# Two feed-forward openings re-ordered: a third pair by quarters, a down product set sooner, and t1, norm sums and one weight part at other times

## The chip, the cores and the metric

The kernel runs on one core of a Trainium2 chip. The metric is the device time of one execution in microseconds (us). Before the change it is 949.35 us, the median of three runs (948.52 to 949.43). Engines are called as in the profile: PE (matmul) with PEld (its weight loads), DVE (vector), ACT (scalar), POOL (GpSimd, which here issues the transfers that add), SP (which issues all other loads). Each engine works through its own queue in order.

## The reference

One block of an encoder over 512 positions and a width of 1024, in float32:

```python
h = x
h = h + 0.5 * swiglu(rmsnorm(h, g1), ffn1_w_in, ffn1_w_out)     # width 2816
z = rmsnorm(h, gm) @ w_in                                       # conv | q k v r | gate
h = h + concat([conv_module(z), gated_linear_attention(z)]) @ w_out
h = h + 0.5 * swiglu(rmsnorm(h, g2), ffn2_w_in, ffn2_w_out)     # width 2816
h = h + sigmoid(rmsnorm(h, gp) @ w_gate) * (p @ w_proj)
out = rmsnorm(h, gf)

def swiglu(x, w_in, w_out):
    gate, up = split(x @ w_in, 2)
    return (silu(gate) * up) @ w_out
```

The change is in the two feed-forward parts. "First layer" means the first of them (ffn1), "second layer" the other (ffn2).

## The kernel before

**Numbers in two parts.** Every operand of a matmul is split into a high part (rounded to fp32r by ACT: `high`, `act.copy`) and a low part (the remainder, a subtraction on DVE: `low`). A product takes three matmuls: high by high, high by low, low by high (`mm3`, `mul`). A weight tile of 128 x 1024 thus costs one ACT cast (wh) and one DVE subtraction (wl). `added` and `add_part` make the low part without DVE: ACT writes the negated high part, and a transfer issued by POOL adds the raw weight to it in memory.

**Pairs.** The 2816 columns of the gate and up projections are cut into 11 pairs of 256 (class `Left` holds the weights of one pair: raw tiles a11, a12 for the gate, a21, a22 for the up projection, each 4 of the 8 row blocks). A pair is computed in one of two ways. *Plain*: eight units h0 to h7 of 12 matmuls with 512 columns each (`plain_unit`). *By quarters*: the input rows and weights are cut in four, and seven products replace eight (`m1` to `m7`, 24 matmuls of 256 columns each). This takes sums of weights (s1 and s2 in `s12`, then `s3_`, `s4_`, all on DVE), parts of seven weight operands, and sums of the input called t1 to t4. The inputs' sums are made once per layer by `Right.steps`, and split once per layer in high and low by `Right.split`: two ACT casts and two DVE subtractions of 128 x 512 for each of t1, t2 and t3, and four of each at 128 x 256 for t4. m6 uses t2, m7 t3, m5 t1 and m4 t4.

**Down products.** The pairs' results go into the down projection by cuts of 4 column blocks (two pairs); the first cut takes blocks 0 to 3, thus pairs 0 and 1. A cut is four pieces of 24 matmuls with 512 columns (`second`, `piece`). Each piece works through its blocks in order, twice, and so needs the high and low parts of the activations (actH, actL, made in `act_parts`) of both pairs. An `act_parts` is emitted behind the unit after the pair's last one.

**Order of the work.** PE, DVE and ACT run in the order in which the program emits their instructions (`Ordered`, `in_order(True)`), so that a waiting instruction holds up everything behind it on its engine. In `ffn` a list of units is made (`units`, `add`, `due`), and `drive` walks through it: ahead of unit n it emits the jobs that units further on have asked for (fetches 7 to 9 units ahead, weight sums 6, weight parts `AHEAD` = 4), then the first left-over of the unit before, then the unit itself with its hook (`hooks`: here the splits of t1 to t4 and the steps of the input's sums hang), then the other left-overs. The raw weights, the wh and the wl have six buffers each, PSUM seven banks for this.

In the first layer pair 0 is computed at the kernel's start, pairs 1 and 2 are plain (`plain` = (1, 2)), and pairs 3 to 10 go by quarters. The list before starts

```text
h0..h7 of pair 1 | h0 h1 h2 | piece 0 | h3 | piece 1 | h4 h5 | piece 2 | h6 h7 | piece 3 (pair 2) | m1 3, m2 3, m1 4, m6 3, ...
```

and t2, t3, t1, t4 are split behind h5 and h7 of pair 1, h3 of pair 2 and m1 of pair 3. In the second layer pair 0 is plain and written out by hand ahead of `ffn` (`plain_block`: g0, u0, g1_, u1_, 24 matmuls each); between the blocks stand the input's sums, the norm (`norm.rows()`: eight tiny matmuls that sum the squares, then a chain over DVE and POOL), and the first parts of pair 1's weights. Pairs 1 to 10 go by quarters.

Of the kernel before, what the change touches and what calls it, by code (L numbers as in the profile page):

```python
# [62 lines left out]
def block_kernel(ctx: ExitStack, tc: tile.TileContext, a: dict, out: bass.AP):  # L63
# [29 lines left out]
    def tmp(s, w=SEQ, dt=F32, bufs=2):  # L93
        return tp.tile([P, w], dt, tag=s, bufs=bufs, name=nm(s))

    def bank():
        return pp.tile([P, SEQ], F32, tag="mm", bufs=7, name=nm("ps"))

    def aux():
        return pp.tile([P, SEQ], F32, tag="aux", bufs=1, name=nm("ax"))  # L100
# [108 lines left out]
    def mm3(ps, wh, wl, xh, xl, first, last):  # L209
        pe.matmul(ps, wh, xh, start=first, stop=False)  # L210
        pe.matmul(ps, wh, xl, start=False, stop=False)
        pe.matmul(ps, wl, xh, start=False, stop=last)
# [46 lines left out]
    def spread(col, copy=True):  # L259

        ps = aux()
        for j in range(TB):
            pe.transpose(ps[:, j * P:(j + 1) * P], col[:, j:j + 1].to_broadcast([P, P]), ident)
        if not copy:
            return ps
        bc = tmp("bc", bufs=1)
        act.copy(bc, ps)
        return bc
# [17 lines left out]
    class Norm:  # L286
# [5 lines left out]
        def add(self, h):  # L292
            if self.n == 0:
                act.activation(self.acc, h, AF.Square)
            else:
                sq = tmp("sq", bufs=3)
                act.activation(sq, h, AF.Square)
                self.engine.tensor_tensor(out=self.acc, in0=self.acc, in1=sq, op=ALU.add)
            self.n += 1
# [214 lines left out]
    w1 = Left(ffn1_in, 2)  # L514
# [9 lines left out]
    ps0 = [bank() for _ in range(4)]  # L524
    split_w(0, 1, dve.tensor_copy)
    split_x(0)
    mid = []
# [22 lines left out]
    xb = Right(hg, "ffn1_norm")  # L550
# [31 lines left out]
    AHEAD = 4  # L582
# [18 lines left out]
        for f in left:  # L601
            f()

    def ffn(w_in, w_out, x, gname, given, first, rsb, hooks, plain):


        norm = Norm()
# [3 lines left out]
        start = 1 + len(plain)  # L611
# [82 lines left out]
        def plain_unit(j):  # L694

            up, i, k = j // 4, j // 2 % 2, j % 2
            def run(p):
                if not j:
                    p.g, p.s = {}, {}
                if not k:  # L700
                    p.x = bank()
                ps = p.x
                wh, wl = p.part(f"a{1 + up}{1 + k}")
                cs = slice(i * P, (i + 1) * P)
                for c in range(4):
                    mm3(ps, wh[:, c, cs], wl[:, c, cs], *x.rows[4 * k + c], k == c == 0, k == 1 and c == 3)
                if not k:
                    return []
                if not up:
                    def gate():  # L710
                        p.s[i] = silu(scaled(ps, "g1"))
                    return [gate]
                return [lambda: gated_block(p, p.s[i], scaled(ps, "u1"), i),
                        lambda: act_parts(p) if i else None]
            return run
# [4 lines left out]
        def unit(kind, i):  # L720
            p = pairs[i]

            def go(run):
                left = run(p)
                hooks.get((kind, i), lambda *_: None)()
                return left

            if kind[0] == "h":
                j = int(kind[1])
                part, run = (f"a{1 + j // 4}{1 + j % 2}", plain_unit(j)) if j % 4 < 2 else (None, plain_unit(j))  # L730
                if part:
                    return [(AHEAD, lambda: p.part(part)), (9, lambda: p.fetch(part))], lambda: go(run)
            else:
                part, run = USES[kind]
            before = [(AHEAD + (kind == 'm5'), lambda: p.part(part))] if part else []
            if kind in ("m1", "m2"):
                before.append((7, lambda: p.fetch(part)))
            elif kind == "m6":
                before += [(9, lambda: p.fetch("a21", "a22")), (6, p.s12)]
            elif kind in ("m7", "m3"):  # L740
                before.append((6, p.s3_ if kind == "m7" else p.s4_))

            return before, lambda: go(run)
# [61 lines left out]
        units, had = [], set()  # L805

        def add(kind, i):
            if 0 <= i < npair and (kind, i) not in had:
                had.add((kind, i))
                units.append(unit(kind, i))  # L810

        cut_of = {f1 // 2 - 1: (f0, f1) for f0, f1 in CUTS}
        due = []
        for i in plain:
            for j in range(8):
                add(f"h{j}", i)
                if j in (2, 3, 5, 7):
                    units += due[:1]
                    due = due[1:]
            if i in cut_of:  # L820
                due += second(cut_of[i])
        for unit_ in (("m1", start), ("m2", start), ("m1", start + 1)):
            add(*unit_)
        for i in range(start, npair):
            add("m6", i)
            add("m7", i)
            add("m5", i)
            if i == end:
                half, rest = second(cut_of[i])
                units.append(half[0])  # L830
            else:
                add("m1", i + 1)
            add("m2", i + 1)
            units += due[:1]
            add("m4", i)
            add("m3", i)
            units += due[1:2]
            due = due[2:]
            if i in cut_of and i < end:
                due += second(cut_of[i])  # L840
        units += half[1:] + rest
# [18 lines left out]
    w_in = a["w_in"][0]  # L860
    w_ahead = []

    def sums_hooks(x, names, at):

        h = {}
        for name, key in zip(names, at):
            h[key] = lambda *_, name=name: x.split(name)
        return h

    hooks = sums_hooks(xb, ("t2", "t3", "t1", "t4"), (("h5", 1), ("h7", 1), ("h3", 2), ("m1", 3)))  # L870
    hooks.update({("h%d" % (i + 1), 1): f for i, f in enumerate(steps[2:])})
    hooks.update({("m5", 3): lambda *_: made[0](), ("m5", 4): lambda *_: constants(),
                  ("m4", 10): lambda *_: w_ahead.append(ahead(w_in, D_CONV, 2 * P)),
                  ("last", 4): lambda *_: w_ahead.append(ahead(w_in, 0, 2 * P))})
    hg, norm = ffn(ffn1_in, a["ffn1_w_out"][0], xb, "mix_norm", {0: Left(ffn1_in, 0), 1: w1},
                   (ps0[:2], ps0[2:]), lambda: spread(mid[0]), hooks, (1, 2))
    pool.on = False
    cw, gwu, mean, mask, nbias = made

# [61 lines left out]
    mid = []  # L941
# [10 lines left out]
    rs, rsb = mid  # L952
# [16 lines left out]
    for k0 in range(0, DC, 4):  # L969
        for i in range(2):  # L970
            for j in range(4):
                pe.matmul(ps[2 * RANK * j:2 * RANK * (j + 1)], gw[:, k0 + j, :], hg[k0 + j][i].bitcast(F32),
                          start=(k0 == i == 0), stop=(k0 + i == 5), skip_group_check=True)
# [339 lines left out]
    w0, w1 = wf[0], wf[1]  # L1313
# [40 lines left out]
    norm = Norm()  # L1354
# [36 lines left out]
    def turn_p(k):  # L1391
        ps = aux()
        for t in range(TB):
            pe.transpose(ps[:, t * P:(t + 1) * P], ptok[t][:, k * P:(k + 1) * P], ident)
        hi, lo = bt(F32R, "pTH"), bt(F32R, "pTL")
        act.copy(hi, ps)
        dve.tensor_tensor(out=lo, in0=ps, in1=hi.bitcast(F32), op=ALU.subtract)
        pT.append((hi, lo))
# [15 lines left out]
    def plain_block(p, up, i, mid={}):  # L1414
        ps = bank()
        cs = slice(i * P, (i + 1) * P)
        for k in range(DC):
            if k in mid:
                mid[k]()
            wh, wl = p.part(f"a{1 + up}{1 + k // 4}")  # L1420
            mm3(ps, wh[:, k % 4, cs], wl[:, k % 4, cs], *hg[k], k == 0, k == DC - 1)
        return ps

    mid = []
    xb = Right(hg, "ffn2_norm")
# [3 lines left out]
    w2 = wf[2]  # L1429
# [1 line left out]
    g0 = plain_block(w0, 0, 0)  # L1431
    steps[1]()
    steps[2]()
    u0 = plain_block(w0, 1, 0, {2: lambda: mid.append(norm.rows())})
    steps[3]()
    w1.add_part("a11", "a12")
    steps[4]()
# [1 line left out]
    g1_ = plain_block(w0, 0, 1, {1: lambda: mid.append(spread(mid[0]))})  # L1439
    xb.split("t2", "t3")  # L1440
    w1.part("s2")
    w1.s3_()
    w1.add_part("a22")
    u1_ = plain_block(w0, 1, 1)
    w1.part("s3")
    hooks = sums_hooks(xb, ("t1", "t4"), (("m1", 1), ("m2", 1)))
    hooks.update({("m7", 10): lambda *_: turn_p(0), ("m5", 10): lambda *_: turn_p(1)})

    w_gate = a["ple_w_gate"][0]
    q11, q21, q12, q22, b11, b21, t2, wproj = ([] for _ in range(8))  # L1450
# [59 lines left out]
    def todo(*fs):  # L1510
# [6 lines left out]
                  ("rest", 4): todo((q_high, b21, q21, 1), (first_sum, 1), (third_sum, 1)),  # L1517
                  ("rest", 6): todo((final_in,), (row_sums, 0))})
    hg, norm = ffn(ffn2_in, a["ffn2_w_out"][0], xb, "ple_norm", wf, ((g0, u0), (g1_, u1_)), mid[1], hooks, ())

    def of_rows(k, h):

        return [tuple(t[:, HS[h]] for t in hg[4 * k + c]) for c in range(4)]

    a11, a12, a21, a22 = of_rows(0, 0), of_rows(1, 0), of_rows(0, 1), of_rows(1, 1)
# [138 lines left out]
    def kept(ps, name, **kw):  # L1666
        o = tmp(name, **kw)
        act.copy(o, ps)
        return o
# [20 lines left out]
    t1, t3 = q11, q12  # L1690
    n2_ = [x for jp in range(2) for x in split_rows(n2, jp)]
    project(0)
    m1 = [kept(p_, "sq", bufs=3) for p_ in x_]
# [98 lines left out]
```

## Time and profile before

| | |
|---|---|
| median of three runs | 949.35 us |
| profiled execution | 949.29 us |
| its span, first to last instruction | 947.6 us |
| PE busy | 935.2 us (99%) |
| DVE busy | 758.0 us (80%) |
| ACT busy | 474.9 us (50%) |
| POOL busy | 55.4 us (6%) |
| mean granted PE clock | 0.998 |

In the timeline's rows the first number is the start in us, the second the time that the row covers, then engine, line, operation, tiles (out<-in), shapes, how many instructions are merged, and in square brackets the idle time before them and what ended it. Nearly all instructions are recorded at line 46, which is the helper that emits them, so they are told apart by tile names. A matmul's modelled duration overlaps the next one's; the rate is read from the starts.

### The profile page before, as it was taken

How to read it: one execution, taken by the hardware profiler on the slowest of the kernel's cores; microseconds unless marked ns; L12 is line 12 of the kernel's file. 1: busy time of each engine (PE TensorE's matmuls, PEld its weight loads, DVE VectorE, ACT ScalarE, POOL GpSimd, SP SyncE). 2: the span in 40 equal slices, each digit the busy share in tenths (PEclk: the TensorE clock that was granted, in tenths of full speed). 3: DMA queues.
4: the chain of work that ended last, by engine and by line, in shares of the span. 5: the costliest groups of instructions: out<-in, count | busy, mean ns of one | idle time of the engine just before them, and what ended most of it. 6: DMA issues, size and time to landing. Idle time of an engine off the chain costs nothing.

```text
span 947.6 us, 14550 instructions
## 1 busy us (share of the span) xinstructions
PE 935.2 (99%) x5842; PEld 831.2 (88%) x5842; DVE 758.0 (80%) x1032; ACT 474.9 (50%) x718; POOL 55.4 (6%) x70
## 2 busy tenths in 40 slices
PE   9999999999999999999999999999999999999996
PEld 7888999999999988788877789999999999998885
DVE  5876887887788566999986789887878787866896
ACT  5752544334443474463564865444434433445883
POOL 0000200000000110001120010000000000000121
PEclk9999999999999999999999999999999999999999
DMA  7532323342323593346552552432243224347463
GB/s 230 180 114 74 103 70 120 101 134 79 101 89 111 142 261 80 76 118 151 134 133 78 146 134 67 126 108 79 89 135 112 67 90 134 95 148 224 89 108 115
DMA packets 107543, 112.38 MB, mean 119 GB/s; under 512 B 5123, under 2 KB 96437, under 8 KB 107476
## 3 DMA queue, kind: packets, MB, share of 16 engines
q1 hardware_dynamic: 101732, 94.67, 32.3%
q0 software_dynamic: 5728, 16.78, 9.9%
q8 instruction: 46, 0.75, 0.3%
q14 instruction: 21, 0.17, 0.0%
q10 hardware_dynamic: 16, 0.00, 0.0%
HBM read 93.61 MB, written 2.10 MB: 101 GB/s over the span
## 4 chain that ended last, share of the span: by engine, by line
PE 96%; DVE 3%; ACT 1%; issue 0%; POOLq 0%; POOL 0%; DVEq 0%; ACTq 0%
PE ps L46 94%; PE ax L46 2%; DVE sqacc L46 1%; DVE wl L46 1%; DVE g L46 0%; DVE wr L46 0%; ACT wh L46 0%; DVE hgL L46 0%; ACT s L46 0%; DVE y L46 0%; DVE t1L L46 0%; POOLq L1788 0%; DVE actL L46 0%; ACT ycH L46 0%; ACT hgH L46 0%
## 5 line engine op out<-in xcount | busy, mean ns | idle before, releaser
L46 PE MATMUL ps<-hgH,wh 128*128 128x256 f32 (+1 forms) x768 | 235.8, 312 | 0.0
L46 PE MATMUL ps<-hgH,wl 128*128 128x256 f32 (+1 forms) x768 | 234.0, 310 | 0.9 <-DVE wl L46 0.9
L46 PE MATMUL ps<-hgL,wh 128*128 128x256 f32 (+1 forms) x768 | 234.2, 310 | 0.0
L46 DVE TENSOR_TENSOR wl<-wr,wh 128x1024 fp32r<-128x1024 f32 (+2 forms) x164 | 192.1, 1182 | 49.4 <-ACT wh L46 49.3
L46 ACT CAST wh<-wr 128x1024 fp32r<-128x1024 f32 (+2 forms) x177 | 177.8, 1019 | 32.8 <-PE ps L46 18.5
L46 PEld LDWEIGHTS ps<-hgH,wh 128*128 128x128 f32 x768 | 146.9, 191 | 9.9 <-issue 1.1
L46 PEld LDWEIGHTS ps<-hgH,wl 128*128 128x128 f32 x768 | 146.6, 191 | 8.7 <-DVE wl L46 1.1
L46 PEld LDWEIGHTS ps<-hgL,wh 128*128 128x128 f32 x768 | 146.3, 191 | 8.1 <-issue 0.2
L46 PE MATMUL ps<-actH,wh 128*128 128x512 f32 x352 | 137.4, 390 | 0.0
L46 PE MATMUL ps<-actL,wh 128*128 128x512 f32 x352 | 137.3, 390 | 0.0
L46 PE MATMUL ps<-actH,wl 128*128 128x512 f32 x352 | 136.9, 389 | 0.0
L46 ACT ACTIVATE s<-g 128x512 f32<-128x512 f32 x48 | 30.4, 633 | 196.1 <-DVE g L46 196.1
L46 DVE SCALAR_TENSOR_TENSOR cv<-glu,cw,cv 128x502 f32<-128x502 f32 (+24 forms) x120 | 81.0, 732 | 0.6
L46 PEld LDWEIGHTS ps<-actH,wl 128*128 128x128 f32 x352 | 66.1, 188 | 13.9
L46 PEld LDWEIGHTS ps<-actH,wh 128*128 128x128 f32 x352 | 66.2, 188 | 12.9
L46 PEld LDWEIGHTS ps<-actL,wh 128*128 128x128 f32 x352 | 66.2, 188 | 12.6
L46 DVE SCALAR_TENSOR_TENSOR h<-ps,h 128x512 f32<-128x512 f32 x80 | 54.0, 687 | 21.8 <-PE ps L46 21.8
L46 ACT COPY sq<-ps 128x512 f32<-128x512 f32 x40 | 23.3, 584 | 72.2 <-PE ps L46 72.2
L46 DVE TENSOR_TENSOR wl<-sm,wh 128x1024 fp32r<-128x1024 f32 x40 | 48.7, 1221 | 1.5 <-ACT wh L46 1.2
L46 ACT CAST wh<-sm 128x1024 fp32r<-128x1024 f32 x40 | 41.8, 1044 | 7.2 <-DVE sm L46 3.9
L46 ACT CAST actH<-m 128x512 fp32r<-128x512 f32 x44 | 25.4, 618 | 38.1 <-DVE m L46 38.0
L46 PE MATMUL ps<-t1H,wh 128*128 128x256 f32 x144 | 40.9, 284 | 0.4 <-ACT u L46 0.4
(267 smaller groups left out, 1740.7 us busy)
## 6 DMA issues: line engine op xcount, KB each, us to landing
wr<-in_ffn_w_in SPq DMA_DIRECT2D x84, 512.0 KB
wr<-in_ffn_w_out SPq DMA_DIRECT2D x32, 512.0 KB
wr<-in_w_in SPq DMA_DIRECT2D x20, 512.0 KB
wl<-wr POOLq DMA_DIRECT2D x14, 512.0 KB, 5.4
wr<-in_ffn_w_out SPq DMA_DIRECT2D x16, 384.0 KB
wr<-in_w_out SPq DMA_DIRECT2D x8, 512.0 KB
wq<-in_ple_w_gate SPq DMA_DIRECT2D x8, 512.0 KB
wl<-wq POOLq DMA_DIRECT2D x8, 512.0 KB, 4.8
```

The source lines that it names most:

```text
L46: inst = call(*args, **kwargs)
```

## The change

In the first layer:

- `plain` becomes (1,): the third pair (number 2) goes by quarters.
- The first piece of the down product (`sooner`) is put right behind m2 of pair 2, ahead of m1 of pair 3. The other three pieces come behind m3 of pair 2, ahead of m4 of pair 3 and behind m3 of pair 3.
- t2, t3, t1, t4 are split behind h4, h5 and h6 of pair 1 and m1 of pair 2.
- Three weight parts are made by `add_part` (ACT and a POOL transfer) and not on DVE: a21 of pair 1, a11 and a22 of pair 2. For a11 and a22 the job stands 6 units ahead.

The new list starts

```text
h0..h7 of pair 1 | m1 2, m2 2 | piece 0 | m1 3 | m6 2, m7 2, m5 2, m2 3, m4 2, m3 2 | piece 1 | m6 3, m7 3, m5 3, m1 4, m2 4 | piece 2 | m4 3, m3 3 | piece 3 | ...
```

In the second layer:

- The norm's sums stand ahead of the fifth k of u0 and not of the third.
- a11 of pair 2 is made by `add_part` ahead of u1_, and not on DVE four units ahead of its use; a22 of pair 1 changes places with the sum s3.
- t1 is split behind u1_, ahead of the part of s3, and not behind m1 of pair 1; t4 stays behind m2 of pair 1.

```diff
-    def ffn(w_in, w_out, x, gname, given, first, rsb, hooks, plain):
+    def ffn(w_in, w_out, x, gname, given, first, rsb, hooks, plain, adds=()):
...
                 if part:
-                    return [(AHEAD, lambda: p.part(part)), (9, lambda: p.fetch(part))], lambda: go(run)
+                    make = p.add_part if (kind, i) in adds else p.part
+                    return [(AHEAD, lambda: make(part)), (9, lambda: p.fetch(part))], lambda: go(run)
             else:
                 part, run = USES[kind]
-            before = [(AHEAD + (kind == 'm5'), lambda: p.part(part))] if part else []
+            if (kind, i) in adds:
+                before = [(AHEAD + 2, lambda: p.add_part(part))]
+            else:
+                before = [(AHEAD + (kind == 'm5'), lambda: p.part(part))] if part else []
...
-        for unit_ in (("m1", start), ("m2", start), ("m1", start + 1)):
-            add(*unit_)
+        add("m1", start)
+        add("m2", start)
+        sooner, due = due[:1], due[1:]
+        units += sooner
+        add("m1", start + 1)
...
-            units += due[:1]
+            if not (i == start and sooner):
+                units += due[:1]
+                due = due[1:]
             add("m4", i)
             add("m3", i)
-            units += due[1:2]
-            due = due[2:]
+            units += due[:1]
+            due = due[1:]
...
-    hooks = sums_hooks(xb, ("t2", "t3", "t1", "t4"), (("h5", 1), ("h7", 1), ("h3", 2), ("m1", 3)))
+    hooks = sums_hooks(xb, ("t2", "t3", "t1", "t4"), (("h4", 1), ("h5", 1), ("h6", 1), ("m1", 2)))
...
-                   (ps0[:2], ps0[2:]), lambda: spread(mid[0]), hooks, (1, 2))
+                   (ps0[:2], ps0[2:]), lambda: spread(mid[0]), hooks, (1,),
+                   {("h4", 1), ("m1", 2), ("m4", 2)})
...
-    u0 = plain_block(w0, 1, 0, {2: lambda: mid.append(norm.rows())})
+    u0 = plain_block(w0, 1, 0, {4: lambda: mid.append(norm.rows())})
...
     w1.part("s2")
+    w1.add_part("a22")
+    w2.add_part("a11")
     w1.s3_()
-    w1.add_part("a22")
     u1_ = plain_block(w0, 1, 1)
+    xb.split("t1")
     w1.part("s3")
-    hooks = sums_hooks(xb, ("t1", "t4"), (("m1", 1), ("m2", 1)))
+    hooks = sums_hooks(xb, ("t4",), (("m2", 1),))
```

## The prediction

> **What bounds the kernel now.** I read the page first, then the chain that ended last, then the timeline of PE, DVE and ACT around the two places that the change touches.
>
> ```profile
> span 947.6 us, 14550 instructions
> PE 96%; DVE 3%; ACT 1%; issue 0%; POOLq 0%; POOL 0%; DVEq 0%; ACTq 0%
> ```
>
> The path is PE nearly everywhere. A change gains only where it takes matmul time away or closes a gap between matmuls, and it loses where it makes PE wait. In the first layer's opening PE has no gap at all. These two rows are the first matmul of pair 2 (h0) and, after three plain units of 12 matmuls, the first of piece 0 of the down product:
>
> ```profile
> 54.37 0.39 PE L46 MATMUL ps<-hgH,wh 128*128 128x512 f32 x1
> 62.53 0.39 PE L46 MATMUL ps<-actH,wh 128*128 128x512 f32 x1
> ```
>
> 36 matmuls in 8.16 us: 0.2267 us for one of 512 columns. The second layer's opening is the one place where PE does wait, three times:
>
> ```profile
> 544.06 1.02 PE L46 MATMUL ax<-ones,sqacc 128*128 128x1 f32 x8 [0.65 <-DVE sqacc L46]
> 567.78 0.39 PE L46 MATMUL ps<-hgH,wl 128*128 128x256 f32 x1 [0.94 <-DVE wl L46]
> 576.82 0.39 PE L46 MATMUL ps<-t1H,wh 128*128 128x256 f32 x1 [0.38 <-ACT u L46]
> ```
>
> **The change, first layer.** *Matmuls.* Consecutive matmuls of 256 columns, 46 apart:
>
> ```profile
> 560.50 0.28 PE L46 MATMUL ps<-hgH,wh 128*128 128x256 f32 x1
> 566.01 0.28 PE L46 MATMUL ps<-hgL,wh 128*128 128x256 f32 x1
> ```
>
> 5.51 us / 46 = 0.1198 us, so a unit m takes 24 x 0.1198 = 2.88 us. Pair 2 plain is 96 x 0.2267 = 21.76 us; by quarters it is 168 x 0.1198 = 20.13 us. Term: **-1.63 us**.
>
> *What stands ahead of piece 0.* Piece 0 needs pair 1's activations at its third block. PE now comes there behind m1 2 and m2 2 and not behind three plain units: 54.37 + 2 x 2.88 + 6 x 0.2267 = 61.49 us, and its second matmul, the one that reads actL, at 61.72. Before it was 62.53 + 1.36 + 0.23 = 64.12. This is the DVE queue before, from pair 1's last weight part to these activations; every instruction is in the order of the program:
>
> ```profile
> 42.39 1.22 DVE L46 TENSOR_TENSOR wl<-wr,wh 128x1024 fp32r<-128x1024 f32 x1 [0.26 <-ACT wh L46]
> 43.54 2.14 DVE L46 TENSOR_TENSOR xg<-xg,xg 128x512 f32<-128x512 f32 x3
> ...
> 48.94 2.15 DVE L46 TENSOR_TENSOR xg<-xg,xg 128x512 f32<-128x512 f32 x3 [2.07 <-ACT xg L46]
> 51.00 1.22 DVE L46 TENSOR_TENSOR wl<-wr,wh 128x1024 fp32r<-128x1024 f32 x1
> 52.13 0.68 DVE L46 TENSOR_TENSOR g<-ps,bc 128x512 f32<-128x512 f32 x1
> 54.52 1.23 DVE L46 TENSOR_TENSOR wl<-wr,wh 128x1024 fp32r<-128x1024 f32 x1 [1.70 <-ACT wh L46]
> 55.66 1.29 DVE L46 TENSOR_TENSOR t2L<-xg,t2H 128x512 fp32r<-128x512 f32 x2
> 56.87 0.68 DVE L46 TENSOR_TENSOR u<-ps,bc 128x512 f32<-128x512 f32 x1
> ...
> 58.20 1.22 DVE L46 TENSOR_TENSOR wl<-wr,wh 128x1024 fp32r<-128x1024 f32 x1
> 59.33 1.28 DVE L46 TENSOR_TENSOR t3L<-xg,t3H 128x512 fp32r<-128x512 f32 x2
> 60.54 0.68 DVE L46 TENSOR_TENSOR u<-ps,bc 128x512 f32<-128x512 f32 x1
> ...
> 61.86 1.46 DVE L46 TENSOR_TENSOR actL<-m,actH 128x512 fp32r<-128x512 f32 x2
> ```
>
> The reader is to see that before, actL came only about 1.5 us ahead of need (61.86 + 0.69 = 62.55 against 64.12), and that DVE was busy for nearly all that stretch (waits of 2.07 and 1.70 us). The sizes of two further steps stand later in the same queue: s1 and s2 from 87.82 to 90.21, and t4's four from 102.17 to 103.51.
>
> ```profile
> 87.82 1.22 DVE L46 TENSOR_TENSOR sm<-wr,wr 128x1024 f32<-128x1024 f32 x1
> ...
> 90.21 1.22 DVE L46 TENSOR_TENSOR wl<-wr,wh 128x1024 fp32r<-128x1024 f32 x1
> ...
> 102.17 1.43 DVE L46 TENSOR_TENSOR hgL<-xg,hgH 128x256 fp32r<-128x256 f32 x4
> 103.51 1.22 DVE L46 TENSOR_TENSOR wr<-wr,sm 128x1024 f32<-128x1024 f32 x1
> ```
>
> Now walk through the new list. The left-over of h7 that makes actL is emitted behind m1 2 and its hook. Ahead of it come, by their distances, s12 of pair 2 (six ahead of m6 2, so at h6), s3 (at h7), the parts a11 of pair 3 (at h7, four ahead of m1 3) and s2 of pair 2 (at m1 2), and the splits of t1 (behind h6) and t4 (behind m1 2). None of these stood ahead of it before. In their place only a11 of pair 2 (the wl at 51.00) leaves; a12 of pair 2 and piece 0's part keep their places. DVE: s12 2.39 + s3 1.14 + two wl at 1.14 + t1 1.20 (as t2's 55.66 to 56.87) + t4 1.34 - 1.13 = **7.2 us more**. If the two waits stay as long, actL starts at 61.86 + 7.2 = 69.1 and block 2 is ready at 69.1 + 0.69 = 69.8. PE wants it at 61.72, so it waits **8.1 us**. If the added work filled both waits (3.77 us), the wait would be 4.3 us; that is the lower end, since the instructions themselves can't be shorter. I take 8.1: the waits come from ACT's turn (silu, then cast) behind each g, which stays. The upper end is 9.0, for one ping-pong with ACT more (0.9, about a cast).
>
> Behind the waiting matmul stand 17 matmuls of piece 0 and all of pair 2's units. What is late next: nothing that I find. DVE goes on during PE's wait and has s1 and s3 (2 x 1.14) by 73, while PE gets to m7 2 at 69.8 + 3.9 + 2 x 2.88 = 79.5. Later in the layer the order is the old one.
>
> *ACT and POOL.* The three parts by transfer cost ACT one more pass each, of the length of this row's, and the first stands ahead of the copy of bc, before which ACT idled:
>
> ```profile
> 35.50 0.59 ACT L46 COPY bc<-ax 128x512 f32<-128x512 f32 x1 [0.65 <-PE ax L46]
> 545.85 1.06 ACT L46 ACTIVATE wl<-wr 128x1024 fp32r<-128x1024 f32 x1
> wl<-wr POOLq DMA_DIRECT2D x14, 512.0 KB, 5.4
> ```
>
> At most 1.06 - 0.65 = 0.4 us go into the chain ahead of actL; I take 0 within the 8.1. The transfers run beside PE: a21's, issued near 36, lands by the median of that row near 41.4, and h4 starts at 54.37 - 4 x 2.72 = 43.5. Were it 3 us late, PE would wait there and that much less at piece 0, because actL is set by DVE alone. POOL has nothing else to do then, and SP's fetches only have to come ahead of DVE, which is late.
>
> *After the wait.* No gap of seven us is in the trace, so the speed at which PE restarts after one is unknown. The nearest rows are those of the kernel's start, where the first four real matmuls of 512 columns take from 6.16 to 7.96:
>
> ```profile
> 1.61 2.40 PE L46 MATMUL ax<-ident 128*128 128x128 f32 x10 [1.61 <-POOL ident masks.py:199]
> ...
> 6.16 1.96 PE L46 MATMUL ps<-hgH,wh 128*128 128x512 f32 x4
> 7.96 1.09 PE L46 MATMUL ps<-hgH,wl 128*128 128x512 f32 x4
> ```
>
> That is 0.45 us each, twice 0.2267, thus 0.9 us lost. The ends are 0 (the second layer's gaps of up to 0.94 us are followed by the full rate) and 3.2, if the whole stretch up to 7.96 from PE's first instruction at 1.61 ran at half speed. I take **+0.9**, the row that it is nearest to.
>
> **The change, second layer.** The rows of DVE and ACT up to the last of the three waits:
>
> ```profile
> 546.68 0.15 DVE L46 TENSOR_SCALAR ms<-ax 128x4 f32<-128x4 f32 x1
> ...
> 559.91 1.22 DVE L46 TENSOR_TENSOR wl<-wr,wh 128x1024 fp32r<-128x1024 f32 x1 [1.17 <-ACT wh L46]
> ...
> 566.51 1.22 DVE L46 TENSOR_TENSOR wl<-wr,wh 128x1024 fp32r<-128x1024 f32 x1
> 567.65 1.29 DVE L46 TENSOR_TENSOR actL<-m,actH 128x512 fp32r<-128x512 f32 x2
> 568.85 1.29 DVE L46 TENSOR_TENSOR t1L<-xg,t1H 128x512 fp32r<-128x512 f32 x2
> ...
> 573.67 0.69 DVE L46 TENSOR_TENSOR g<-ps,sq 128x512 f32<-128x512 f32 x1
> 575.17 0.63 ACT L46 ACTIVATE s<-g 128x512 f32<-128x512 f32 x1 [4.15 <-DVE g L46]
> 576.18 0.59 ACT L46 COPY u<-ps 128x512 f32<-128x512 f32 x1
> ```
>
> The sums two k later (6 x 0.2267 = 1.36 us) close the wait at 544.06, and the norm's rows do not come later: ms waited for DVE's turn until 546.68. So PE runs about 0.8 us earlier up to m1 1. The wait at 567.78 was for the wl at 566.51, which leaves DVE; its transfer can be issued near 559 and lands near 564.5, ahead of m1 2 at about 565.5. But the last wait is for ACT's u, which stands behind silu, which stands behind g at 573.67, at the end of DVE's queue. That queue loses one wl (1.14). t1's two subtractions (1.20) only move ahead; the idle 1.17 at 559.91 gets partly filled by them and partly moves, as ACT has the added cast, the negation and t1's casts ahead of s3's. So u ends 1.14 us earlier and PE, which comes sooner, waits for it longer: the gain is **-1.14 us**, not the sum of the waits. Ends: 0, if t1's place costs DVE what the wl gave; and -1.97, all three waits (0.65 + 0.94 + 0.38).
>
> **Sum.** -1.63 + 8.1 + 0.9 - 1.14 = +6.2 us. The profiled execution took 949.29 us (span 947.6 and 1.7 around it), 0.06 under the median 949.35: both give **955.5 us**.
>
> **The rivals.** *Piece 0 doesn't wait (faster).* If actL were ready in time, -1.63 - 1.14 leaves 946.6 us. It decides at a wait of 2.8 us: actL's first part would have to be ready by 64.5. For it speaks that the list was short of slack before and never stalled; against it, that the DVE work alone, without any wait, ends at 66.0. It would take that I read the places of s12, t1 and t4 wrongly by two units.
>
> *DVE's waits fill up.* A wait of 4.3 us, with no slow restart: -1.63 + 4.3 - 1.14 = +1.5, 950.8 us. Against it: the waits are chains over ACT.
>
> *A slow clock after the gap.* If PE restarts as slowly as in the whole start of the kernel, 3.2 stands in place of 0.9: 957.8 us. For it speaks the 0.45 us of the rows at 6.16; against it that the granted clock is 0.998 over the span and no gap as long is there. The Trainium skill (TensorE: Matmul & The Clock Gate, Part 1: The HAM clock gate) says that an idle window of about 3.4 us brings the array back to half its clock until it was busy for about as long. By that rule the restart costs some 1.7 us, an estimate from that page, and the sum would be 956.3; the doubled times at 6.16 agree with the half rate, no run here shows the gap.
>
> *The second layer gains nothing:* 956.6 us.
>
> **How the numbers follow.** Chances: forecast (953.5 to 956.5, the last rival within it or beside it) 0.60; slow clock 0.18; filled waits 0.12; faster 0.10. The likeliest gives 955.5. The range goes from the filled waits, 950.8, up to the slow clock with part of the second layer's gain lost, 958.5, and leaves out the faster case. No change that can be told is within 0.2% of 949.35, thus 947.45 to 951.25: it gets 0.05, from the filled waits with a little more gain. Faster 0.09, slower 0.86.
>
> **What would show it.** In the profile after: a PE gap of 6 to 9 us near 62, ended by actH or actL; actL near 69; matmuls behind it for a microsecond or more at 0.45; no PE wait for sqacc and none for wl in the second layer's opening, a longer one for u, ended some 1.1 us earlier relative to the layer's start. Wrong it is if actL comes ahead of 64, or if a later unit of the first layer waits too (s4 or a22, landing late).

## The result and the profile after

The changed kernel takes 956.06 us (median of 6 runs, 955.65 to 956.63), the kernel before 949.3 us (6 runs, 948.52 to 950.62). The ratio is 1.0071, with a 95% interval of 1.0058 to 1.0084: slower by 0.7%, as forecast (955.5 us, range 950.8 to 958.5). The profiled execution took 956.29 us against 949.29.

First the page of the changed kernel, its span and the chain that ended last:

```profile
span 954.6 us, 14724 instructions
PE 89%; DVE 4%; DMA 3%; ACT 2%; issue 2%; SPq 1%; POOL 0%; POOLq 0%; DVEq 0%; ACTq 0%
```

PE's share of the chain fell from 96% to 89%. What PE waited for (waits of PE in the changed kernel: us in total, times, longest):

```profile
PE ps L46 <- DVE actL L46: 6.5, 1, 6.5
PE ax L46 <- POOL ident masks.py:199: 1.6, 1, 1.6
PE ps L46 <- DMA wl<-wr: 1.4, 1, 1.4
PE ps L46 <- ACT actH L46: 0.9, 1, 0.9
```

The waits for actH and actL are new, both at piece 0; no wait of PE in the first layer is for a transfer. The three waits of the second layer's opening are gone, and one of 1.4 us for a transfer (wl<-wr, a POOL add) has come. PE's timeline around piece 0 in the changed kernel:

```profile
53.73 0.28 PE L46 MATMUL ps<-hgH,wh 128*128 128x256 f32 x1
...
59.48 0.40 PE L46 MATMUL ps<-actH,wh 128*128 128x512 f32 x1
...
60.64 0.39 PE L46 MATMUL ps<-actH,wl 128*128 128x512 f32 x1
61.91 0.50 PE L46 MATMUL ps<-actH,wh 128*128 128x512 f32 x1 [0.88 <-ACT actH L46]
68.88 0.80 PE L46 MATMUL ps<-actL,wh 128*128 128x512 f32 x1 [6.47 <-DVE actL L46]
69.47 0.63 PE L46 MATMUL ps<-actH,wl 128*128 128x512 f32 x1
69.90 0.63 PE L46 MATMUL ps<-actH,wh 128*128 128x512 f32 x1
...
74.17 0.44 PE L46 MATMUL ps<-actL,wh 128*128 128x512 f32 x1
...
75.38 0.28 PE L46 MATMUL ps<-hgH,wh 128*128 128x256 f32 x1
```

Piece 0 starts at 59.48 and m1 of pair 3 follows at 75.38: 15.9 us for work of 24 x 0.2267 = 5.44. The second matmul of block 2 was due at 60.64 + 2 x 0.2267 = 61.09 and came at 68.88: a wait of **7.8 us**. From 68.88 to 75.38 stand 17 matmuls, 6.50 us where 3.85 were due: **2.65 us** more, because between 69.47 and 74.17 one takes 0.427 us and not 0.227. The next fence is the view by windows (stretch, its length, busy us of PE, PEld, DVE, ACT, POOL with counts, granted clock, DMA share, GB/s; a granted clock of 1.00 is full speed):

```profile
59.00:62.00 3.00, 2.12 (x13) 1.52 (x11) 2.96 (x5) 2.85 (x7) 0.00 (x0) 1.00 0.38 105
62.00:68.80 6.80, 0.41 (x1) 0.09 (x1) 6.77 (x12) 1.88 (x3) 0.00 (x0) 0.65 0.34 108
68.88:74.17 5.29, 5.29 (x13) 4.13 (x13) 4.71 (x6) 3.09 (x4) 0.86 (x1) 0.50 0.17 37
74.17:80.00 5.83, 5.83 (x45) 5.61 (x44) 4.39 (x5) 1.64 (x2) 0.00 (x0) 0.99 0.71 160
```

DVE is busy for 6.77 of the 6.80 us in which PE stands still, and the granted clock behind the gap is 0.50. DVE's queue in that stretch, from t3 to the parts that follow actL:

```profile
54.81 1.28 DVE L46 TENSOR_TENSOR t3L<-xg,t3H 128x512 fp32r<-128x512 f32 x2
56.01 1.22 DVE L46 TENSOR_TENSOR sm<-wr,wr 128x1024 f32<-128x1024 f32 x1
...
60.87 1.28 DVE L46 TENSOR_TENSOR t1L<-xg,t1H 128x512 fp32r<-128x512 f32 x2
62.07 1.22 DVE L46 TENSOR_TENSOR wr<-wr,wr 128x1024 f32<-128x1024 f32 x1
63.21 1.22 DVE L46 TENSOR_TENSOR wl<-wr,wh 128x1024 fp32r<-128x1024 f32 x1
64.34 1.22 DVE L46 TENSOR_TENSOR wl<-sm,wh 128x1024 fp32r<-128x1024 f32 x1
...
66.80 1.42 DVE L46 TENSOR_TENSOR hgL<-xg,hgH 128x256 fp32r<-128x256 f32 x4
68.14 1.28 DVE L46 TENSOR_TENSOR actL<-m,actH 128x512 fp32r<-128x512 f32 x2
```

Ahead of actL stand s12 (sm), t1, s3 (wr), the part a11 of pair 3, s2's part and t4 (hgL), as the walk through the list had it.

**A measure without the start.** The time at which the first layer begins differs from profile to profile by up to 2 us: in these kernels the transposes that spread the first layer's norm start between 34.22 and 36.43. I therefore also compare from these transposes to the last matmul of a quarter product at the kernel's end. The rows of before, then of the changed kernel:

```profile
34.87 0.60 PE L46 MATMUL ax<-ident,rs 128*128 128x128 f32 x4
...
938.77 0.28 PE L46 MATMUL ps<-wl,sH 128*128 128x256 f32 x1
```

```profile
34.22 0.60 PE L46 MATMUL ax<-ident,rs 128*128 128x128 f32 x4
...
945.79 0.28 PE L46 MATMUL ps<-wl,sH 128*128 128x256 f32 x1
```

903.90 us before, 911.57 after: +7.67. "Norm to end" below is this measure, in one profiled execution each. "First layer" is from the same transposes to the first matmul that sums the squares in the second layer's opening, compared with the kernel that has only the second layer's part (509.78 us): 518.64 in the changed kernel, +8.86, close to the sum of its parts, 7.8 + 2.65 - 1.63 = 8.82. The first layer alone, whose opening of the second layer is the old one, is compared with the kernel before in this (509.19 us). The last column, "from the sums on", is what is left of the norm to the end: the second layer's opening and all behind it.

| kernel | timed ratio to before (95%) | norm to end, us | against before | first layer | from the sums on |
|---|---|---|---|---|---|
| before | | 903.90 | | | |
| changed | 1.0071 (1.0058 to 1.0084) | 911.57 | +7.67 | +8.86 | -1.19 |
| second layer alone | 1.0009 (1.0000 to 1.0018) | 903.88 | -0.02 | 0 | -0.02 |
| first layer alone | 1.0095 (1.0080 to 1.0110) | 912.35 | +8.45 | +8.44 | +0.01 |
| t1, t4 later | 1.0064 (1.0049 to 1.0079) | 908.63 | +4.73 | +5.90 | -1.17 |
| piece 0 not sooner | 1.0086 (1.0069 to 1.0103) | 911.94 | +8.04 | +9.19 | -1.15 |
| filled with matmuls | 1.0053 (1.0038 to 1.0067) | 909.08 | +5.18 | +6.34 | -1.16 |
| filled with transposes | 1.0085 (1.0072 to 1.0098) | 911.46 | +7.56 | +6.37 | +1.19 |
| mended | 1.0031 (1.0019 to 1.0042) | 907.17 | +3.27 | +4.42 | -1.15 |
| mended, adds swapped | 1.0030 (1.0020 to 1.0039) | 905.98 | +2.08 | +3.26 | -1.18 |
| mended again | 1.0048 (1.0035 to 1.0060) | 908.95 | +5.05 | +6.25 | -1.20 |
| second layer, adds swapped | 0.9993 (0.9984 to 1.0003) | 902.67 | -1.23 | -0.03 | -1.20 |
| more adds | 1.0031 (1.0021 to 1.0041) | 907.65 | +3.75 | +4.93 | -1.18 |

### The profile page after: what moved, and what is told of

Same layout as the page of the kernel before. It is cut to its first block, busy times and chain, and to the rows that moved or that the text cites. A ratio compares the mean times of both kernels' runs of the same rounds, so it can differ in the third digit from the quotient of the medians.

```text
span 954.6 us, 14724 instructions
## 1 busy us (share of the span) xinstructions
PE 935.3 (98%) x5914; PEld 834.3 (87%) x5914; DVE 763.4 (80%) x1038; ACT 483.6 (51%) x728; POOL 56.9 (6%) x74
## 4 chain that ended last, share of the span: by engine, by line
PE 89%; DVE 4%; DMA 3%; ACT 2%; issue 2%; SPq 1%; POOL 0%; POOLq 0%; DVEq 0%; ACTq 0%
PE ps L46 88%; PE ax L46 1%; DMA wl<-wr 1%; DMA wr<-in_ffn_w_in 1%; DVE xg L46 1%; DVE wl L46 1%; DMA x<-in_x 1%; DVE sqacc L46 1%; ACT xg L46 1%; ACT wh L46 0%; DMA gwurow<-in_gate_w_up 0%; SPq L481 0%; ACT s L46 0%; DVE g L46 0%; SPq L446 0%
## 5 line engine op out<-in xcount | busy, mean ns | idle before, releaser
L46 PE MATMUL ps<-hgH,wl 128*128 128x256 f32 (+1 forms) x768 | 230.6, 305 | 1.4 <-DMA wl<-wr 1.4
L46 PE MATMUL ps<-hgH,wh 128*128 128x256 f32 (+1 forms) x768 | 231.5, 307 | 0.2 <-DVE wh L46 0.2
L46 PE MATMUL ps<-hgL,wh 128*128 128x256 f32 (+1 forms) x768 | 230.8, 306 | 0.0
L46 DVE TENSOR_TENSOR wl<-wr,wh 128x1024 fp32r<-128x1024 f32 (+2 forms) x161 | 188.6, 1182 | 46.6 <-ACT wh L46 46.5
L46 DVE TENSOR_TENSOR wl<-sm,wh 128x1024 fp32r<-128x1024 f32 x42 | 51.0, 1220 | 1.8 <-ACT wh L46 1.6
L46 DVE TENSOR_TENSOR u<-ps,sq 128x512 f32<-128x512 f32 x19 | 13.1, 691 | 39.3 <-ACT sq L46 39.3
```

What stands on the lines that cost most here:

```text
L46: inst = call(*args, **kwargs)
```

## The experiments

Theory: all of the loss is in the first layer, where DVE's fixed order puts 7.2 us of added work ahead of pair 1's actL, which piece 0 now needs sooner; behind the gap PE restarts at half its clock. Rivals: the second layer carries part of it; the time is spread over pair 2's units or comes from the adds; the slow matmuls have another cause than the gap.

### The two layers apart

Second layer alone:

```diff
-    hooks = sums_hooks(xb, ("t2", "t3", "t1", "t4"), (("h4", 1), ("h5", 1), ("h6", 1), ("m1", 2)))
+    hooks = sums_hooks(xb, ("t2", "t3", "t1", "t4"), (("h5", 1), ("h7", 1), ("h3", 2), ("m1", 3)))
...
-        sooner, due = due[:1], due[1:]
+        sooner = []
...
-    ... hooks, (1,), {("h4", 1), ("m1", 2), ("m4", 2)})
+    ... hooks, (1, 2))
```

> The second layer's part of the change alone, the first layer as before. Theory (the added time is all in the first layer; the second layer's chain over DVE lost one weight part of 1.14 us): 948.2 us, 1.1 under the kernel before. Rival (the second layer's opening adds a late POOL transfer and gains nothing): 949.3 or more.

Measured: 1.0009, and -0.02 us from norm to end. The rival is right here: the opening gains nothing. PE waits 2.56 us at m1 of pair 2 for the POOL add of a11, issued at 559.17 (timeline of PE, then of POOL, this kernel):

```profile
568.23 0.39 PE L46 MATMUL ps<-hgH,wl 128*128 128x256 f32 x1 [2.56 <-DMA wl<-wr]
```

```profile
557.27 0.86 POOL L46 DMA_DIRECT2D wl<-wr  x1 [7.43 <-ACT wl L46]
559.17 0.86 POOL L46 DMA_DIRECT2D wl<-wr  x1 [1.03 <-ACT wl L46]
```

It landed some 9 us after its issue, and the add of a22, which is needed later, was issued 1.9 us ahead of it.

First layer alone: the second layer's lines as before.

```diff
-    u0 = plain_block(w0, 1, 0, {4: lambda: mid.append(norm.rows())})
+    u0 = plain_block(w0, 1, 0, {2: lambda: mid.append(norm.rows())})
...
     w1.part("s2")
-    w1.add_part("a22")
-    w2.add_part("a11")
     w1.s3_()
+    w1.add_part("a22")
     u1_ = plain_block(w0, 1, 1)
-    xb.split("t1")
     w1.part("s3")
-    hooks = sums_hooks(xb, ("t4",), (("m2", 1),))
+    hooks = sums_hooks(xb, ("t1", "t4"), (("m1", 1), ("m2", 1)))
```

> The first layer's part of the change alone, the second layer as before. Theory: 957.2 us, 1.1 above the changed kernel: matmuls -1.6, a PE wait of 7.8 us at piece 0 for actL, and about 2.6 us lost at half the clock behind it. Rival (both layers carry part of the loss): under 955.5.

Measured: 957.69 us, ratio 1.0095; norm to end +8.45, 0.78 above the changed kernel. So the loss is the first layer's. The second layer's part gives more than these 0.78 us in the changed kernel: 1.19 from the sums on. Its add landed sooner there than in the second layer alone, 7.9 us after its issue, and PE's wait for it only takes the place of the wait for ACT's u that stands in the kernel with the adds swapped: from the sums to the end the two take 392.93 and 392.92 us (PE, changed kernel, then the second layer with the adds swapped, which comes further down):

```profile
575.45 0.39 PE L46 MATMUL ps<-hgH,wl 128*128 128x256 f32 x1 [1.39 <-DMA wl<-wr]
```

```profile
576.70 0.38 PE L46 MATMUL ps<-t1H,wh 128*128 128x256 f32 x1 [1.39 <-ACT u L46]
```

The other 0.4 us between the two kernels lie in the first layer, whose instructions are the same in both. Behind a wait as long for actL, the 17 matmuls of piece 0 took 6.04 us in this profile and not 6.50 (PE, first layer alone):

```profile
71.01 0.79 PE L46 MATMUL ps<-actL,wh 128*128 128x512 f32 x1 [6.48 <-DVE actL L46]
...
77.05 0.28 PE L46 MATMUL ps<-hgH,wh 128*128 128x256 f32 x1
```

So the cost of the slow stretch is not a fixed number: 2.65 us in the one profile, 2.19 in the other.

### Is it DVE's order?

```diff
-    hooks = sums_hooks(xb, ("t2", "t3", "t1", "t4"), (("h4", 1), ("h5", 1), ("h6", 1), ("m1", 2)))
+    hooks = sums_hooks(xb, ("t2", "t3", "t1", "t4"), (("h4", 1), ("h5", 1), ("m1", 3), ("m6", 2)))
```

> The changed kernel with t1 split behind m1 of pair 3 and t4 behind m6 of pair 2, so that 1.20 + 1.34 = 2.5 us of DVE work leave the queue ahead of pair 1's actL. Theory (DVE's order sets the wait, one to one): the PE wait at piece 0 falls from 7.8 to 5.3 us; as that is still a long gap the half clock behind it stays, so 953.5 us; if the loss at half clock shrinks with the gap, 952.7. Rival (PE waits at piece 0 for something else, or the time is spread over the layer): the gap stays near 7.8 and the time near 956.1.

PE at piece 0 in this kernel:

```profile
62.33 0.39 PE L46 MATMUL ps<-actH,wl 128*128 128x512 f32 x1
63.34 0.50 PE L46 MATMUL ps<-actH,wh 128*128 128x512 f32 x1 [0.62 <-ACT actH L46]
68.03 0.79 PE L46 MATMUL ps<-actL,wh 128*128 128x512 f32 x1 [4.18 <-DVE actL L46]
```

The matmul due at 62.33 + 0.45 = 62.78 came at 68.03: a wait of 5.25 us, 2.5 less for 2.54 us of DVE work taken away. That is one to one, and the rival of another releaser falls. The half clock stays, but ends sooner (at 71.2, after 3.2 us), which saves another 0.9 us; a new wait for DVE's u at 88.38 takes about 0.5 back, and the first layer is 2.96 us better than in the changed kernel. The timed 955.18 us is 0.9 us under the changed kernel and 1.7 above what was expected. In the profiled execution the first layer started 1.7 us later than in that of the changed kernel; where it started in the other timed runs is not recorded.

### Is it the place of piece 0?

```diff
-        sooner, due = due[:1], due[1:]
+        sooner = []
```

> The changed kernel with piece 0 of the down product ahead of m4 of pair 2 and not behind m2 of pair 2; the rest of the pieces follow by one place. Theory (the place of the piece against the DVE queue is what costs, but that queue is late for the quarters too): no wait for actL; instead m6 2 waits some 2 to 3 us for s2's low part and m7 2 or m5 2 another 2 to 3 us for s3's or s1's, each too short for the half clock, so about 950 us (948.5 to 951.5). Rival (the piece's place alone costs everything): all of 10.4 us come back, 945.7 us.

Both expectations missed: 957.11 us, first layer +9.19. Piece 0 doesn't wait, and the parts a11 of pair 3 and s2 cost only 0.9 us (waits of 0.34 and 0.53). The wait has moved to m5 of pair 2, for ACT's copy u, which reads m6's sum ahead of m5 (timeline of PE, then of ACT):

```profile
76.64 0.58 PE L46 MATMUL ps<-t1H,wh 128*128 128x256 f32 x1 [6.46 <-ACT u L46]
```

```profile
67.97 0.62 ACT L46 CAST actH<-m 128x512 fp32r<-128x512 f32 x1 [5.06 <-DVE m L46]
...
74.05 0.63 ACT L46 ACTIVATE s<-g 128x512 f32<-128x512 f32 x1 [2.62 <-DVE g L46]
...
76.00 0.59 ACT L46 COPY u<-ps 128x512 f32<-128x512 f32 x1
```

ACT stood 5.06 us at the second actH, for DVE's m, and 2.62 us at silu, for DVE's g; the copy is behind both in ACT's queue. So the piece's place only decides at which matmul PE meets DVE's lateness. Setting it sooner isn't what costs.

### The slow matmuls behind the gap

```diff
                             f = f0 + k
+                            if adds and f == 2 and n == i == 0:
+                                fill, idle = x.rows[4][0], aux()
+                                for _ in range(30):
+                                    pe.matmul(idle, fill[:, 0:P], fill, start=True, stop=True)
                             mm3(
```

> The changed kernel with 30 matmuls of 512 columns, whose product nobody reads, put on PE just ahead of piece 0's third block: about 6.8 us of PE work inside the wait of 7.8 us. Theory (the doubled matmul times behind the wait come from PE's idleness): the remaining gap is about 1 us, the granted clock stays at 1.0 behind it and piece 0's matmuls keep 0.227 us: 2.6 us less than the changed kernel, about 953.5. Rival (the slow matmuls come from the operands or from contention, not from idleness): no gain, 956.

```diff
+                            if adds and f == 2 and n == i == 0:
+                                warm_up(64)
```

> As the fill with matmuls, but with 64 transposes of 128 x 128 (about 0.1 us each, 6.4 us). If transposes keep the clock up as matmuls do: about 953.5. If the clock doesn't count them as activity: half clock behind the wait as in the changed kernel, about 956.

With matmuls PE reaches actL with 0.8 us to wait, and the matmuls behind it keep their 0.23 us (PE, filled with matmuls):

```profile
70.80 0.50 PE L46 MATMUL ps<-actL,wh 128*128 128x512 f32 x1 [0.82 <-DVE actL L46]
71.14 0.40 PE L46 MATMUL ps<-actH,wl 128*128 128x512 f32 x1
71.37 0.39 PE L46 MATMUL ps<-actH,wh 128*128 128x512 f32 x1
```

The first layer is 2.52 us better than in the changed kernel, close to the 2.65 measured as the slow stretch. So it is PE's idleness that the slow matmuls come from. The transposes do the same: first layer +6.37 against +6.34. That the timed ratio with transposes is no better than the changed kernel's has another place: in that kernel's second layer the wait for the add was 2.27 us, and behind it the granted clock fell to 0.75 in the five us from 575 (from the sums on +1.19).

### A version without the wait

The units on PE as changed, DVE's work for pair 2 put behind actL:

```diff
+            near = bool(adds) and i == start
...
-                before = [(AHEAD + (kind == 'm5'), lambda: p.part(part))] if part else []
+                far = AHEAD + (kind == 'm5')
+                if near and kind in ("m6", "m7", "m5") or adds and (kind, i) == ("m1", start + 1):
+                    far = 3 if kind == "m5" else 2
+                before = [(far, lambda: p.part(part))] if part else []
...
-                before += [(9, lambda: p.fetch("a21", "a22")), (6, p.s12)]
+                before += [(9, lambda: p.fetch("a21", "a22")), (3 if near else 6, p.s12)]
...
-                before.append((6, p.s3_ if kind == "m7" else p.s4_))
+                before.append((3 if near and kind == "m7" else 6, p.s3_ if kind == "m7" else p.s4_))
...
-    ... (("h4", 1), ("h5", 1), ("h6", 1), ("m1", 2)))
+    ... (("h4", 1), ("m2", 2), ("m1", 3), ("m6", 2)))
```

> The changed kernel with the same units on PE, but with DVE's work ahead of pair 1's actL taken down: t3, t1, t4 split behind m2 of pair 2, m1 of pair 3 and m6 of pair 2; s12 and s3 of pair 2 three units ahead of their use and not six; the parts s2, s3 and a11 of pair 3 two ahead, s1 three. That moves 9.5 us of DVE work behind actL. Theory: actL comes at about 58.6 against a need of 61, no PE wait, no half clock, only the 1.63 us fewer matmuls are left beside what the second layer gives (0 to 0.8): 947.3 us. Rival (DVE is then late for m7 2 or m5 2, or ACT's copy of m6 2 stands behind a waiting cast): 949 to 952.

The second kernel of this kind has the two adds of the second layer in the other order as well:

```diff
-    w1.add_part("a22")
     w2.add_part("a11")
+    w1.add_part("a22")
```

> The mended kernel with the two POOL adds of the second layer's opening in the other order: a11 of pair 2 (needed first) ahead of a22 of pair 1. Theory (in the second layer PE now waits for the second of two adds in flight, which lands 8 to 9 us after its issue): the add is issued 1.6 to 1.9 us sooner and alone, lands before m1 2, no PE wait for it; the bound is then DVE's queue, 1.1 us better than before the change: about 946.4 us, 0.4 to 1.1 under the mended kernel. Rival (the landing doesn't depend on the order, or a22 becomes late for m4 1): no better than the mended kernel.

Mended: 951.62 us, 4.4 under the changed kernel and 2.3 above the one before; the rival's range. actL came in time and piece 0 didn't wait. But m7 of pair 2 did, first for s3's cast and then for its low part (PE, mended with the adds swapped, then DVE in the same kernel):

```profile
72.48 0.38 PE L46 MATMUL ps<-t3H,wh 128*128 128x256 f32 x1 [1.08 <-ACT wh L46]
...
74.72 0.38 PE L46 MATMUL ps<-t3H,wl 128*128 128x256 f32 x1 [1.73 <-DVE wl L46]
```

```profile
59.13 1.46 DVE L46 TENSOR_TENSOR actL<-m,actH 128x512 fp32r<-128x512 f32 x2
60.51 1.22 DVE L46 TENSOR_TENSOR sm<-wr,wr 128x1024 f32<-128x1024 f32 x1
...
73.44 1.22 DVE L46 TENSOR_TENSOR wl<-wr,wh 128x1024 fp32r<-128x1024 f32 x1
```

From 54.19 to 82.93 DVE has no gap in its queue there. The two short waits also brought the half clock, for longer in the one profile than in the other (windows of the mended kernel, then of the one with the adds swapped):

```profile
75.00:80.00 5.00, 3.70 (x17) 3.70 (x18) 4.97 (x10) 3.21 (x9) 0.00 (x0) 0.55 0.36 105
80.00:85.00 5.00, 5.00 (x35) 5.00 (x34) 4.60 (x4) 1.28 (x2) 0.00 (x0) 0.77 0.28 88
```

```profile
75.00:80.00 5.00, 5.00 (x31) 5.00 (x31) 4.97 (x9) 2.65 (x5) 0.00 (x0) 0.66 0.34 105
```

Swapping the adds took the wait for the transfer away (1.42 us), and one of 1.38 us for ACT's u came in its place: from the sums on the two kernels differ by 0.03 us. Of the 1.19 us between them from norm to end (907.17 to 905.98), 1.16 lie in the first layer, where their instructions are the same and the slow matmuls went on to 82.2 in the one profile and to 79.2 in the other. So the swap gained nothing here, as the timed ratios say, and the rival is right.

The third attempt mends the order of s3 and gives a11 of pair 3 to a POOL add. In it s3 overwrites a21 before s1 reads it, so that three of pair 2's seven products (m5, m6 and m3, by s1, s2 and s4) are of other sums; the sizes of the instructions are the same.

```diff
-                before.append((3 if near and kind == "m7" else 6, p.s3_ if kind == "m7" else p.s4_))
+                before.append(((4 if kind == "m7" else 5) if near else 6, p.s3_ if kind == "m7" else p.s4_))
...
-                if near and kind in ("m6", "m7", "m5") or adds and (kind, i) == ("m1", start + 1):
-                    far = 3 if kind == "m5" else 2
+                if near and kind in ("m6", "m7", "m5"):
+                    far = 2 if kind == "m6" else 3
...
-                   {("h4", 1), ("m1", 2), ("m4", 2)})
+                   {("h4", 1), ("m1", 2), ("m4", 2), ("m1", 3)})
```

> The mended kernel with the two adds swapped, and three further moves of DVE work in the first layer: the part s3 of pair 2 one unit sooner (it came last of four jobs and PE waited 1.7 us for it, and 1.1 us for its cast), s4 of pair 2 one unit later, and a11 of pair 3 made by a POOL add and not on DVE. Theory: no PE wait is left in the first layer's opening, 1.63 us of matmuls are gone and the second layer gives 1.1: 946.0 us, so under the kernel before (948.5 to 949.4) by 0.25 to 0.35%. Rival (with DVE full up to m5 2 the next part is late instead, s1 or t1): 947.5 to 950.

953.61 us: missed. s3 was in time, and PE waited 3.5 us for DVE's u, which reads m5's result and stands behind the sums and parts of the next pair in DVE's queue. The fourth gives six more parts than the mended kernel to POOL adds, and moves the parts of s1 and s4, s3 and s4 as well (against the mended kernel with the adds swapped):

```diff
-                if near and kind in ("m6", "m7", "m5") or adds and (kind, i) == ("m1", start + 1):
-                    far = 3 if kind == "m5" else 2
+                if near and kind in ("m6", "m7", "m5", "m3"):
+                    far = 3 if kind == "m3" else 2
...
-                before.append((3 if near and kind == "m7" else 6, p.s3_ if kind == "m7" else p.s4_))
+                before.append(((3 if kind == "m7" else 5) if near else 6, p.s3_ if kind == "m7" else p.s4_))
...
-                    got[f0, n, g] = parts(got[f0, n, g])
+                    make_ = (lambda r3: added(high(r3))[:2]) if adds and f0 == 0 and n else parts
+                    got[f0, n, g] = make_(got[f0, n, g])
...
-                   {("h4", 1), ("m1", 2), ("m4", 2)})
+                   {("h4", 1), ("m1", 2), ("m4", 2), ("m2", 2), ("m1", 3), ("m2", 3)})
```

> The mended kernel with the two adds of the second layer swapped, s3 of pair 2 made three units ahead, its part two ahead, s1's part two ahead, s4 one unit later, and six more weight parts of the first layer's opening made by POOL adds and not on DVE (a12 of pair 2, a11 and a12 of pair 3, the parts of pieces 1 to 3 of the first cut): 6.8 us of DVE work less up to piece 3. Theory (what is left of the loss is DVE's load between pair 1 and pair 3, in whatever order it stands): the PE waits in the first layer's opening fall under 1 us in all, and with 1.63 us fewer matmuls and 1.2 us of the second layer's opening the kernel is 2 to 2.8 us under the one before, from the first layer's norm to the end: about 946.7. Rival (the adds land late, or ACT's second pass takes the place of DVE's): PE waits for a transfer or for ACT, 949 to 952.

952.31 us, missed as well. Four waits for DVE are left (waits of PE):

```profile
PE ps L46 <- DVE u L46: 2.3, 1, 2.3
...
PE ps L46 <- DVE wl L46: 1.4, 3, 0.8
```

DVE now stands still in places where it waits for ACT's second pass (2.07 us ahead of piece 0's part), and ACT waits 3.79 us for piece 1's weights, which landed 5.0 us behind their issue and not 3.5 as in the mended kernel with the adds swapped. So part of what DVE gave up came back as waits for ACT and for loads. Behind the wait of 2.3 us the granted clock fell to 0.53 as well (86.4 to 90.0). Whether any order makes pair 2 by quarters worth its 1.63 us stays open: none of the four did.

### The second layer with the adds swapped

```diff
     w1.part("s2")
-    w1.add_part("a22")
     w2.add_part("a11")
+    w1.add_part("a22")
     w1.s3_()
```

> The second layer's part of the change alone, with a11 of pair 2 added ahead of a22 of pair 1; the first layer as before. Theory (the late landing of the second add took the gain): no PE wait for an add; PE waits about 1.4 us for ACT's u instead, which comes 1.1 us sooner than before the change: 1.1 us under the kernel before, measured from the first layer's norm to the end. Rival (the landing is as late in either place): no gain, as with the second layer alone.

From norm to end -1.23 us, as expected, with no wait for a transfer and one of 1.4 us for ACT's u. The timed ratio, 0.9993 (0.9984 to 1.0003), can't tell it from no change: 1.2 us is 0.13%, and the start of the kernel alone moves by more. It is the best kernel of the study by the trace, and not shown faster by the timed runs. Whether the old order of the adds costs anything differs from profile to profile: with the same instructions in the second layer, the add landed 7.9 us after its issue in the changed kernel, at no cost, 8.7 us after it in the kernel filled with transposes, and 9.0 in the second layer alone, where it took the whole gain. Of the two adds the first landed after 5.5 us in the second layer alone and here as well, though it makes another part in each.

## Why the prediction was right

- *Matmuls, -1.63 us*: right. With the wait and the slow stretch it adds up to 8.82 of the first layer's +8.86.
- *The wait at piece 0, 8.1 us*: 7.8 in the profile; with t1 and t4 later, 2.54 us less of DVE work took 2.5 off it; actL at 68.14, where 69.1 was forecast on a clock that ran 0.64 us later. That the two waits of DVE would stay was nearly right: 1.76 and 1.27 us stand in the queue after, for 2.07 and 1.70. The range's lower end, all waits filled, was not met.
- *The restart, +0.9 us*: the term that was mis-sized; it measured 2.65, and 2.19 in the first layer alone. The mechanism was in the rival "a slow clock after the gap", priced at 3.2 from the whole start, and the fills show it. The row chosen for the 0.9 was the wrong one. The first four matmuls of the kernel, 6.16 to 7.96 before, take 6.35 to 7.35 in the changed kernel, with a granted clock of 1.00 in both, so their slowness was not the clock's. The clock stood at 1.00 from the start of the span, so the rival's 3.2 was read from rows that don't show it either, and that it came nearer is luck. The half clock that the rule of the Trainium skill (TensorE: Matmul & The Clock Gate, Part 1: The HAM clock gate) gives is what the trace shows, 0.50 from 68.88 to 74.17, over 5.3 us and not the 3.4 that made 1.7 us of it. The idle time of that rule isn't borne out: the clock halved behind shorter waits too (see the last section).
- *The second layer, -1.14 us*: the size was right, -1.19 from the sums on in the changed kernel. The step that failed is "its transfer ... lands near 564.5, ahead of m1 2": the add landed 7.9 us after its issue and not 5.4, and PE waited 1.39 us for it there. That this cost nothing rests on the bound that the prediction named, DVE's queue and ACT's u: with the adds swapped PE waits the same 1.39 us for u. Where the add landed after 9.0 us, in the second layer alone, it became the bound and the gain was gone.
- The measured terms, -1.63 + 7.8 + 2.65 - 1.19 = 7.63, agree with the +7.67 from norm to end; the forecast was 6.2. The changed kernel's profile started 0.65 us sooner than that of before, which is chance, so that 7.0 us stand between the profiles and 6.8 between the medians. The nearness of 955.5 to 956.06 is in part luck.
- *Piece 0 doesn't wait (faster)* fell with the 7.8 us. Nor did its price hold where its condition was met: in the mended kernel actL came in time and piece 0 didn't wait, but PE waited at m7 of pair 2 instead, and the kernel took 951.62 us and not 946.6. The prediction tied DVE's lateness to piece 0 alone; with the piece not set sooner it was met at m5.

## What to carry to other kernels

Where each engine's order is fixed, count an engine's work between two points at which the path needs it, and compare it with the time that the path gives; a product with fewer matmuls that asked more of a nearly full vector engine was paid for there in all the orders tried here. A gap of several us on PE cost more than its length, by slow matmuls behind it; matmuls and transposes that nobody reads kept them fast, though they don't shorten the gap. When a weight part is moved from an engine to a transfer, put the transfer that is needed first ahead in its queue, and take its time from transfers that overlap another one. And compare two kernels stretch by stretch: a difference in a stretch whose instructions are the same belongs to the profile and not to the edit.

## What the runs showed of the hardware

The granted clock halved behind gaps much shorter than the one in question: behind 2.27 us in the second layer (filled with transposes), behind 2.26 us (more adds), and behind 1.07 and 1.74 us with 0.5 us of matmuls between them (mended, clock 0.55 in the five us from 75). Behind 2.56 us in the second layer alone it didn't (1.00 from 568.2 to 573). So the length of a gap alone doesn't decide, and what else does stays open. Nor does it decide how long the half clock lasts: behind the same two short waits the slow matmuls cost 1.1 us more in one profile than in another. Transposes of 128 x 128, 64 in 6.9 us, kept the clock at 1.00 as matmuls did. A POOL add of 512 KB that was issued 1.6 to 1.9 us behind another in the second layer's opening landed 7.7 to 9.0 us after its issue, the one ahead of it 5.5 to 5.6, against a median of 5.4 in the kernel before. Elsewhere in the kernel before, an add 1.9 us behind another (issued at 901.63) landed after 5.9 us, and one with no other beside it (at 432.87) after 9.7, so the add ahead is not the only cause of a late landing.
